# RWKV preparation with Y and Q both kept as diagonal blocks and Q's changed columns turned from Y

## The chip, the cores and the metric

The program runs on one core of a Trainium2 chip. The metric is the device time of one execution in microseconds, over several runs. The program is one launch: two layers of a trunk over 1152 tokens (1024 latent tokens and 128 context tokens), held on chip as columns, 384 tokens to a block.

## The reference, cut to what matters

Layer 1 holds a bidirectional RWKV-7 time mixing with 8 heads of 64 channels. Its scan, per head and direction, is

```python
def step(S, inp):
    r_t, w_t, k_t, v_t, kk_t, a_t = inp
    sa = jnp.einsum('bhvk,bhk->bhv', S, -kk_t)
    S = (S * w_t[:, :, None, :] + sa[..., None] * (kk_t * a_t)[:, :, None, :]
         + v_t[..., None] * k_t[:, :, None, :])
    y = jnp.einsum('bhvk,bhk->bhv', S, r_t)
    return S, y
```

The kernel computes it in chunks of 64 tokens. Inside a chunk the term `sa` makes token t depend on all earlier tokens of the chunk through a strictly triangular 64x64 matrix N (its entries are masked products of kk, a and the decay), so each chunk needs the inverse of I - N. All else in the layer around it (projections, mLSTM, norms) is matrix products and elementwise work.

## The kernel before, in words

`odd_layer_mixer` runs layer 1's two mixers. For RWKV it walks 36 steps (4 pairs of heads x 9 chunk groups). One step handles four units: two directions by two chunks of 64 tokens, with two heads on the two halves of the 128 partitions. For each step a generator `prep` (L1292) computes what does not depend on the running state, in 18 pieces divided by `yield`; `chain_block` (L1467) then carries the state. At most two `prep` generators are active, the second nine pieces behind the first. Between pieces the loop (L934 on) calls `topup`, which advances a third generator: the fills, that is the input projections of the layer, their follow-up work, and later the mLSTM. How much fill is issued between two pieces is set by a due time of 0.74 us of matmul work (`DUE`), counted by `Counted` (L53) for the fills alone; matmuls of `prep` count for nothing there. The order in which the program issues pieces is a priority and not the order of execution: the framework places each engine's instructions by readiness and its own costs when the program is closed, so a matmul of one preparation can stand among those of the other. Every matmul is recorded under L67 and every transpose under L71, so groups in the profile are told apart by their tile names.

Inside `prep` the inverse is built by doubling blocks. Y is the inverse so far (block size 1, 2, 4 ... 32), Q is its transpose. Per preparation both live in one f16 tile `YQ`, 64 columns to a unit, the heads in the two halves of the partitions. `DB[bank]` holds three f16 tiles of 128x128 diagonal blocks for the four units: N1 and N2 (the high and low parts of the triangular matrix) and QB (Q as diagonal blocks: head 0 top left, head 1 bottom right, zeros elsewhere). The pieces that concern the change:

- L1315 to L1317: Q is set to the identity. `start_inverse` (L1345): N1 is filled, and the columns that level 0 changes are copied into Q under a mask.
- L1384 to L1388: Q is copied into QB (two ACT copies, one for each half of the partitions), four matmuls with QB give Y (`i,DB` in the rows), ACT copies Y out.
- Each level l from 1 to 5, first piece: four matmuls N1 x Y (`YQ,DB`, 64 columns each), and ACT copies the product from PSUM to R (L1394).
- Each level, second piece: four matmuls QB x R (`R,DB`) give Y's new columns and eight 64x64 matmuls R x Q (`YQ,R`) give Q's. One masked copy on DVE (L1415) puts the changed half of the columns of both into YQ. Up to level 4, two ACT copies then bring Q's changed columns into QB (L1420).
- L1423 to L1431: sixteen matmuls of 64 columns form the correction I - Y + N1 Y + N2 Y; two ACT copies put it into N1 as diagonal blocks.
- L1433 to L1439: eight matmuls of 64 columns form the corrected transpose, and two ACT copies put it into PD, f32, as diagonal blocks.

Next, PD meets AT (`AT,PD`), and the results WT and EF go to the chain. A preparation has PSUM bank `sm0` or `sm1` of its own; `sm3` is shared by both, and `sm2` is the chain's.

Of the kernel before, what the change touches and what calls it, by code (L numbers as in the profile page):

```python
# [15 lines left out]
F16 = mybir.dt.float16  # L16
# [7 lines left out]
P = 128  # L24
# [61 lines left out]
def trunk_kernel(ctx: ExitStack, tc: tile.TileContext, A, outs, dbg=None, upto=99, odd="rm"):  # L86
# [7 lines left out]
    ve, sc, gp, te, sy = nc.vector, nc.scalar, nc.gpsimd, Counted(nc.tensor), nc.sync  # L94
# [13 lines left out]
    def smps(i=None):  # L108

        if i is None:  # L110
            G.turn += 1
            i = G.banks[G.turn % len(G.banks)]
        return ps_sm.tile([P, 512], F32, tag=f"sm{i}", name="sm")
# [685 lines left out]
    CH = 64  # L799
    DECAY = math.exp(-0.5)  # L800
    NCH = NT // P
    HR = [slice(0, 64), slice(64, 128)]
# [3 lines left out]
    def odd_layer_mixer(h, early):  # L806
# [19 lines left out]
        sp1 = s1.enter_context(tc.tile_pool(name="sp1", bufs=1))  # L826
        St = stage1(h, early, w_in, zm, gd, zd, zvt, zbg, zar, zbk, wend, sp1, op)
        Rw = rwkv(zd, zvt, zbg, zar, zbk, wend, y, op, fp)

        started = [0, False]  # L830
# [401 lines left out]
    def rwkv(zd, zvt, zbg, zar, zbk, wend, y, mp, fp):  # L1232
# [8 lines left out]
        i16 = mp.tile([P, CH], F16, tag="i16", name="i16")  # L1241
# [3 lines left out]
        id16 = mp.tile([P, 2, P], F16, tag="id16", name="id16")  # L1245
# [4 lines left out]
        DB = []  # L1250
        for i in range(2):
            t = mp.tile([P, 3, 4, P], F16, tag=f"DB{i}", name="DB")
            gp.memset(t, 0.0)
            DB.append(t)
        PD = mp.tile([P, 4, P], F32, tag="PD", name="PD")
        gp.memset(PD, 0.0)

        AGs = []
        for i in range(2):
            t = mp.tile([P, 4, 6, CH], F32, tag=f"AG{i}", name="AG")  # L1260
# [29 lines left out]
        def prep(n, p, i):  # L1290
            B = block_of(p, i)
            bank = n % 2  # L1292
# [9 lines left out]
            for d in range(2):  # L1302
                for hh, hr in enumerate(HR):
                    src = zvt[p][tb[d], :, hr].rearrange("(c t) v -> t c v", c=2)
# [7 lines left out]
                    gp.memset(B.XV[hr, 0::3, hh], 0.0)  # L1312


            YQ = mp.tile([P, 2, 2, 2, CH], F16, tag="YQ", name="YQ", bufs=2)  # L1315
            Y, Q = YQ[:, :, 0], YQ[:, ::-1, 1]
            sc.copy(Q, i16.unsqueeze(1).unsqueeze(1).to_broadcast([P, 2, 2, CH]))  # L1317
            yield

            GB = mp.tile([P, 4, 3, CH], F32, tag="GB", name="GB", bufs=2)  # L1320
            rights = [cols(AG, hh, PRODUCTS) for hh in range(2)]
            pgs = [smps(bank), smps(3)]
            N1, QB, N2 = (DB[bank][:, j] for j in range(3))
            lower = [GB[:, :, k] for k in ALPHA]

            def level(ap, l, first, stride, parity, dims):


                b = 1 << l
                head = [list(ap.ap[0]), [stride + (parity[1] - parity[0]) * b, 2]]  # L1330
                return bass.AP(tensor=ap.tensor, offset=ap.offset + first + parity[0] * b, ap=head + dims + [[1, b]])

            def lmask(l, hr, n):

                o = 4 * (64 - (64 >> l))
                return lm[hr, :, o : o + n * (32 >> l)].bitcast(mybir.dt.uint16)
# [8 lines left out]
            def start_inverse(hh):  # L1345
                hr = HR[hh]
                sc.copy(N1[hr, :, hr], lower[hh][hr])  # L1347
                dst = level(YQ[hr], 0, 6 * CH, -4 * CH, (1, 0), [[CH, 2], [2, 32]])[:, :, :, :, 0]
                src = level(lower[hh][hr], 0, 0, 6 * CH, (1, 0), [[3 * CH, 2], [2, 32]])[:, :, :, :, 0]
                m = lmask(0, hr, 2)[:, ::-1].rearrange("p j (c k) -> p j c k", c=2)  # L1350
                ve.copy_predicated(dst, m, src)
# [7 lines left out]
            pt = smps(3)  # L1359
            for u in range(4):  # L1360
                te.transpose(pt[:, u * P : u * P + P], BK[:, u], ident)
            for hh in (1, 0):
                start_inverse(hh)
# [4 lines left out]
                sc.copy(AG[ho, :, 5 * hh], ptv[ho, :, hr])  # L1368
            yield

            def mm2(o, lt, rt):
                for u in range(4):
                    d, c = divmod(u, 2)
                    for r_ in (slice(0, P),) if lt.shape[-1] == P else HR:
                        te.matmul(o[r_, d, c], lt[r_, u], rt[r_, d, c], start=True, stop=True)

            def halves_of(ps):
                return ps[:, : 4 * CH].rearrange("p (d c n) -> p d c n", d=2, c=2)

            def u22r(t):  # L1380
                return t.rearrange("p (d c) n -> p d c n", d=2)

            i16b = i16.unsqueeze(1).unsqueeze(1).to_broadcast([P, 2, 2, CH])
            for hr in HR:  # L1384
                sc.copy(u22r(QB)[hr, :, :, hr], Q[hr])
            py = halves_of(smps(bank))
            mm2(py, QB, i16b)
            sc.copy(Y, py)  # L1388
            yield
            for l in range(1, 6):  # L1390
                pr = halves_of(smps(bank))
                mm2(pr, N1, Y)
                R = mp.tile(U4, F16, tag="R", name="R", bufs=2)
                sc.copy(u22r(R), pr)  # L1394
                if l == 2:

                    for hh, hr in enumerate(HR):
                        gp.tensor_tensor(N2[hr, :, hr], lower[hh][hr], N1[hr, :, hr], op=OP.subtract)  # L1398
                elif l == 5:
                    pt = smps(3)  # L1400
                    for u in range(4):
                        te.transpose(pt[:, u * P : u * P + P], AG[:, u, 2:4].rearrange("p w n -> p (w n)"), ident)
                    AT = mp.tile([P, 4, P], F32, tag="AT", name="AT", bufs=1)
                    sc.copy(AT, pt.rearrange("p (u n) -> p u n", u=4))
                yield
                pyq = smps(bank)
                pyv = pyq.rearrange("p (j i c n) -> p j i c n", j=2, i=2, c=2)
                mm2(pyv[:, :, 0], QB, u22r(R))
                for u in range(4):
                    d, c = divmod(u, 2)  # L1410
                    for hr in HR:
                        te.matmul(pyv[hr, 1 - d, 1, c], R[hr, u], Q[hr, d, c], start=True, stop=True)
                dst, src = (level(t, l, 0, 4 * CH, (0, 1), [[2 << l, 4 * (32 >> l)]]) for t in (YQ, pyq))
                m = lmask(l, slice(0, P), 4).unsqueeze(3).to_broadcast([P, 2, 4 * (32 >> l), 1 << l])
                ve.copy_predicated(dst, m, src)  # L1415
                if l < 5:
                    for hr in HR:
                        nb = [2 << l, 32 >> l]
                        dst = level(QB[hr, :, hr], l, 0, 2 * P, (1, 0), [[P, 2], nb])
                        sc.copy(dst, level(YQ[hr], l, 6 * CH, -4 * CH, (1, 0), [[CH, 2], nb]))  # L1420
                yield

            pe = halves_of(smps(bank))  # L1423
            for u in range(4):
                d, c = divmod(u, 2)
                te.matmul(pe[:, d, c], id16[:, 0], i16, start=True, stop=False)
                te.matmul(pe[:, d, c], id16[:, 1], Y[:, d, c], start=False, stop=False)
                te.matmul(pe[:, d, c], N1[:, u], Y[:, d, c], start=False, stop=False)
                te.matmul(pe[:, d, c], N2[:, u], Y[:, d, c], start=False, stop=True)
            for hr in HR:  # L1430
                sc.copy(u22r(N1)[hr, :, :, hr], pe[hr])  # L1431
            yield
            pq = halves_of(smps(bank))  # L1433
            for u in range(4):
                d, c = divmod(u, 2)
                te.matmul(pq[:, d, c], id16[:, 0], Q[:, d, c], start=True, stop=False)
                te.matmul(pq[:, d, c], N1[:, u], Q[:, d, c], start=False, stop=True)
            for hr in HR:
                sc.copy(u22r(PD)[hr, :, :, hr], pq[hr])  # L1439
            yield  # L1440

            pw = smps(bank)
# [65 lines left out]
        def finish(p, i):  # L1508
# [38 lines left out]
            yield  # L1547

        R_.prep, R_.chain_block, R_.finish = prep, chain_block, finish
        return R_  # L1550

# [555 lines left out]
```

## Time and profile before

| What | us |
|---|---|
| median of 3 runs | 3409.84 |
| lowest and highest run | 3403.11, 3419.9 |
| the profiled execution | 3413.79 |
| its span, first to last instruction | 3411.7 |
| PE busy in the span | 3198.1 (94%) |
| DVE busy | 1888.0 (55%) |
| ACT busy | 1348.5 (40%) |
| POOL busy | 853.8 (25%) |

PE is the engine of the matmuls, PEld its weight loads, DVE, ACT and POOL the vector, scalar and general engines. PE's busy time is modelled and pipelined: of a run of matmuls, the distance from one start to the next is what each costs the engine, and the duration of one (about 0.19 us for 64 columns) is its latency. PEclk is the clock that was granted to PE, 1.00 being 2.4 GHz and 0.50 being 1.2 GHz. The matmuls of the preparation run from 1388 to 2460 us of the span.

### The profile page before, as it was taken

The page shows a single profiled execution, that of the slowest core. Times are in us where ns is not written, and L with a number is a line of the kernel's source. Part 1 is how long each engine was busy: PE and PEld are TensorE (multiplying, and loading weights), DVE is VectorE, ACT ScalarE, POOL GpSimd, SP SyncE. Part 2 cuts the span into 40 slices and gives each one's busy share as a digit, 9 for nine tenths or more (in the row PEclk, how much of TensorE's full clock was granted, in tenths as well). Part 3 has the DMA queues.
Part 4 walks back from the last instruction along what each step waited for, and adds up shares of the span by engine and source line. Part 5 has one row for each costly group of instructions (what it writes and reads, how often), then busy time and mean ns, then how long its engine had stood idle before and what let it go on. Part 6 is the DMA issues. An engine that isn't in the chain of part 4 may idle for free. (4 is left out here: it accounts for less than half of the span.)

```text
span 3411.7 us, 55264 instructions
## 1 busy us (share of the span) xinstructions
PE 3198.1 (94%) x21772; PEld 2939.6 (86%) x21772; DVE 1888.0 (55%) x3964; ACT 1348.5 (40%) x2864; POOL 853.8 (25%) x706
## 2 busy tenths in 40 slices
PE   7897999999999998899989899988899999999998
PEld 4775999999999997677777788877699999999998
DVE  6886655555543366567666864467856333333335
ACT  4545341112221144565665565586535111222112
POOL 2332322121111133233232431223223111111112
PEclk9998999999999999899979899999899999999999
DMA  5235412222211123444333432364251111111111
GB/s 215 91 123 174 149 48 84 92 93 87 93 50 44 44 99 112 136 108 111 102 96 105 108 95 80 107 189 137 85 188 38 44 38 44 44 44 38 44 44 75
DMA packets 255141, 315.29 MB, mean 92 GB/s; under 512 B 77138, under 2 KB 198690, under 8 KB 253346
## 3 DMA queue, kind: packets, MB, share of 16 engines
q1 hardware_dynamic: 254882, 311.77, 29.1%
q8 instruction: 171, 2.80, 0.3%
q14 instruction: 88, 0.72, 0.1%
HBM read 250.59 MB, written 61.10 MB: 91 GB/s over the span
## 5 line engine op out<-in xcount | busy, mean ns | idle before, releaser
L67 PE MATMUL mm<-h,w 128*128 128x384 f32 x8808 | 1737.8, 349 | 12.6 <-POOL w L239 4.1
L67 PEld LDWEIGHTS mm<-h,w 128*128 128x128 f32 x8808 | 1552.7, 191 | 65.1 <-issue 27.0
L67 PE MATMUL mm<-uH,w 128*128 128x384 f32 x3072 | 796.2, 338 | 0.0
L239 POOL TENSOR_TENSOR w<-w 128x1024 fp32r<-128x1024 f32 x153 | 370.6, 2422 | 1386.9 <-ACT w L238 1347.4
L238 ACT CAST w<-w 128x1024 fp32r<-128x1024 f32 x211 | 221.0, 1048 | 888.7 <-PE mm L67 843.9
L67 PEld LDWEIGHTS mm<-uH,w 128*128 128x128 f32 x3072 | 557.5, 188 | 2.5 <-issue 2.5
L376 DVE SCALAR_TENSOR_TENSOR x<-mm,mod,x 128x384 f32<-128x384 f32 (+1 forms) x576 | 282.9, 514 | 446.5 <-PE mm L67 446.0
L67 PE MATMUL mm<-uL,w 128*128 128x384 f32 x1536 | 518.0, 337 | 0.0
L396 DVE SCALAR_TENSOR_TENSOR s<-mm,r 128x384 f32<-128x384 f32 x192 | 106.8, 557 | 403.9 <-ACT r L394 403.8
L67 PEld LDWEIGHTS mm<-uL,w 128*128 128x128 f32 x1536 | 288.6, 188 | 0.0
L394 ACT ACTIVATE r<-mm 128x384 f32<-128x384 f32 x192 | 93.5, 488 | 275.2 <-PE mm L67 274.5
L239 DVE TENSOR_TENSOR uL<-s,uH 128x384 fp32r<-128x384 f32 x192 | 149.8, 781 | 87.6 <-ACT uH L238 87.2
L67 PEld LDWEIGHTS <-DB 128*128 128x128 f16 x2016 | 111.4, 101 | 77.0 <-issue 57.1
L238 ACT CAST uH<-s 128x384 fp32r<-128x384 f32 x192 | 98.5, 513 | 144.8 <-DVE s L396 144.6
L1415 DVE CAST_PREDICATED YQ<-lm,sm 128x256 f16<-128x256 uint16 x180 | 77.1, 428 | 134.8 <-PE sm L67 111.4
L196 DVE SCALAR_TENSOR_TENSOR modacc<-wmod,csl,modacc 128x512 f32<-128x512 f32 x168 | 135.3, 852 | 5.0 <-DMA wmod<-in_w_mod_dram 4.7
L1420 ACT COPY DB<-YQ 64x128 f16<-64x128 f16 x288 | 85.0, 295 | 85.0 <-DVE YQ L1415 81.1
L239 DVE TENSOR_TENSOR w<-w 128x1024 fp32r<-128x1024 f32 x58 | 82.0, 1421 | 54.9 <-ACT w L238 50.9
L67 PE MATMUL sm<-YQ,DB 128*128 128x64 f16 x1152 | 89.0, 198 | 17.6 <-DVE YQ L1415 11.7
L288 POOL TENSOR_TENSOR nacc<-nacc,nsq 128x384 f32<-128x384 f32 x56 | 66.5, 1195 | 146.8 <-ACT nsq L287 111.0
L1398 POOL TENSOR_TENSOR DB<-GB,DB 64x256 f16<-64x256 f32 x72 | 49.0, 680 | 210.4 <-ACT DB L1347 206.1
L67 PEld LDWEIGHTS sm<-XV,EF 128*128 128x128 f32 x576 | 80.0, 204 | 21.6 <-DVE EF L1456 14.9
(352 smaller groups left out, 3792.2 us busy)
## 6 DMA issues: line engine op xcount, KB each, us to landing
w<-in_mlp_w_dram SPq DMA_DIRECT2D x128, 512.0 KB
wmod<-in_w_mod_dram SPq DMA_DIRECT2D x80, 512.0 KB
w<-in_od_w_in_dram SPq DMA_DIRECT2D x31, 512.0 KB
w<-in_od_w_out_dram SPq DMA_DIRECT2D x24, 512.0 KB
BK<-zbk SPq DMA_DIRECT2D x72, 128.0 KB
AG<-zar SPq DMA_DIRECT2D x144, 64.0 KB
hbig<-zm SPq DMA_DIRECT2D x18, 512.0 KB
rb<-rowd SPq DMA_DIRECT2D x36, 256.0 KB
```

Of the source, the lines that this page charges most:

```text
L67: return self.eng.matmul(out, left, right, **kw)
L196: ve.scalar_tensor_tensor(acc[:, s], wm[:, i], c, acc[:, s], op0=OP.mult, op1=OP.add)
L238: sc.copy(Hout, src)
L239: eng.tensor_tensor(Lout, src, Hout.bitcast(F32), op=OP.subtract)
L288: (eng or (ve if tb == NTB - 1 else gp)).tensor_add(self.acc[tb], self.acc[tb], sq)
L376: ve.scalar_tensor_tensor(xs, ps[:, o], modcol(l, 2 if which == 1 else 5, m, s), xs, op0=OP.mult, op1=OP.add)
L394: sc.activation(r, ps[:, :TB], AF.Relu)
L396: ve.scalar_tensor_tensor(s, ps[:, :TB], 0.0, r, op0=OP.max, op1=OP.mult)
L1398: gp.tensor_tensor(N2[hr, :, hr], lower[hh][hr], N1[hr, :, hr], op=OP.subtract)
L1415: ve.copy_predicated(dst, m, src)
L1420: sc.copy(dst, level(YQ[hr], l, 6 * CH, -4 * CH, (1, 0), [[CH, 2], nb]))
```

## The change

Y is kept as diagonal blocks too (`YB`, 128x128 to a unit, f16), and QB is Q's only place; the tile YQ is gone. Q is set to the identity directly in QB by one 128x512 copy, and level 0's masked copy writes into QB. In each level the first piece multiplies N1 by the columns of YB that the level will change alone (again 64 columns a unit, now picked with a stride). Q's changed columns are no longer products of their own: from level 2 on, four more matmuls in the first piece (`turn`, YB as weights, columns of the identity as the moving side) transpose the columns of Y that the level before changed, into the second half of the same PSUM tile, and one ACT copy (`turned`) puts them into QB. The last level's turn stands with the correction, in bank `sm3`. The second piece keeps the four QB x R matmuls and the masked copy, of the same size as before (half of the columns of all 128 of a unit, and not half of 64 twice). The correction and the corrected transpose have 128 columns a matmul, and each is copied out by one ACT copy of 128x512 and not by two of 64x256. PD is written whole, and so the clearing of it is left out. The number of `yield`s is the same.

```diff
@@ -1253,7 +1253,6 @@
             gp.memset(t, 0.0)
             DB.append(t)
         PD = mp.tile([P, 4, P], F32, tag="PD", name="PD")
-        gp.memset(PD, 0.0)
 
         AGs = []
         for i in range(2):
@@ -1312,15 +1311,15 @@
                     gp.memset(B.XV[hr, 0::3, hh], 0.0)
 
 
-            YQ = mp.tile([P, 2, 2, 2, CH], F16, tag="YQ", name="YQ", bufs=2)
-            Y, Q = YQ[:, :, 0], YQ[:, ::-1, 1]
-            sc.copy(Q, i16.unsqueeze(1).unsqueeze(1).to_broadcast([P, 2, 2, CH]))
+
+            N1, QB, N2 = (DB[bank][:, j] for j in range(3))
+            YB = mp.tile([P, 4, P], F16, tag="YB", name="YB", bufs=2)
+            sc.copy(QB, id16[:, 0].unsqueeze(1).to_broadcast([P, 4, P]))
             yield
 
             GB = mp.tile([P, 4, 3, CH], F32, tag="GB", name="GB", bufs=2)
             rights = [cols(AG, hh, PRODUCTS) for hh in range(2)]
             pgs = [smps(bank), smps(3)]
-            N1, QB, N2 = (DB[bank][:, j] for j in range(3))
             lower = [GB[:, :, k] for k in ALPHA]
 
             def level(ap, l, first, stride, parity, dims):
@@ -1345,7 +1344,7 @@
             def start_inverse(hh):
                 hr = HR[hh]
                 sc.copy(N1[hr, :, hr], lower[hh][hr])
-                dst = level(YQ[hr], 0, 6 * CH, -4 * CH, (1, 0), [[CH, 2], [2, 32]])[:, :, :, :, 0]
+                dst = level(QB[hr, :, hr], 0, 0, 2 * P, (1, 0), [[P, 2], [2, 32]])[:, :, :, :, 0]
                 src = level(lower[hh][hr], 0, 0, 6 * CH, (1, 0), [[3 * CH, 2], [2, 32]])[:, :, :, :, 0]
                 m = lmask(0, hr, 2)[:, ::-1].rearrange("p j (c k) -> p j c k", c=2)
                 ve.copy_predicated(dst, m, src)
@@ -1368,30 +1367,44 @@
                 sc.copy(AG[ho, :, 5 * hh], ptv[ho, :, hr])
             yield
 
-            def mm2(o, lt, rt):
+            def columns(t, l, parity):
+
+                return t.rearrange("p (g k b) -> p g k b", k=2, b=1 << l)[:, :, parity]
+
+            def changed(t, l, parity):
+
+                return level(t, l, 0, 2 * P, parity, [[2 << l, 4 * (32 >> l)]])
+
+            def mm4(o, lt, rt):
                 for u in range(4):
-                    d, c = divmod(u, 2)
-                    for r_ in (slice(0, P),) if lt.shape[-1] == P else HR:
-                        te.matmul(o[r_, d, c], lt[r_, u], rt[r_, d, c], start=True, stop=True)
-
-            def halves_of(ps):
-                return ps[:, : 4 * CH].rearrange("p (d c n) -> p d c n", d=2, c=2)
-
-            def u22r(t):
-                return t.rearrange("p (d c) n -> p d c n", d=2)
-
-            i16b = i16.unsqueeze(1).unsqueeze(1).to_broadcast([P, 2, 2, CH])
-            for hr in HR:
-                sc.copy(u22r(QB)[hr, :, :, hr], Q[hr])
-            py = halves_of(smps(bank))
-            mm2(py, QB, i16b)
-            sc.copy(Y, py)
+                    r = rt(u)
+                    n = o.shape[-1] // 4
+                    te.matmul(o[:, u * n : u * n + n], lt[:, u], r, start=True, stop=True)
+
+            def by_unit(t):
+                return t.rearrange("p (u n) -> p u n", u=4)
+
+            def turn(o, l):
+
+                mm4(o, YB, lambda u: columns(id16[:, 0], l, 1 - u // 2))
+
+            def turned(o, l):
+                sc.copy(changed(QB, l, (1, 0)), o.rearrange("p (j g b) -> p j g b", j=2, b=1 << l))
+
+            H = 4 * CH
+            py = smps(bank)
+            mm4(py, QB, lambda u: id16[:, 0])
+            sc.copy(YB, by_unit(py))
             yield
             for l in range(1, 6):
-                pr = halves_of(smps(bank))
-                mm2(pr, N1, Y)
+                ps = smps(bank)
+                mm4(ps[:, :H], N1, lambda u: columns(YB[:, u], l, u // 2))
+                if l > 1:
+                    turn(ps[:, H:], l - 1)
                 R = mp.tile(U4, F16, tag="R", name="R", bufs=2)
-                sc.copy(u22r(R), pr)
+                sc.copy(R, by_unit(ps[:, :H]))
+                if l > 1:
+                    turned(ps[:, H:], l - 1)
                 if l == 2:
 
                     for hh, hr in enumerate(HR):
@@ -1403,40 +1416,29 @@
                     AT = mp.tile([P, 4, P], F32, tag="AT", name="AT", bufs=1)
                     sc.copy(AT, pt.rearrange("p (u n) -> p u n", u=4))
                 yield
-                pyq = smps(bank)
-                pyv = pyq.rearrange("p (j i c n) -> p j i c n", j=2, i=2, c=2)
-                mm2(pyv[:, :, 0], QB, u22r(R))
-                for u in range(4):
-                    d, c = divmod(u, 2)
-                    for hr in HR:
-                        te.matmul(pyv[hr, 1 - d, 1, c], R[hr, u], Q[hr, d, c], start=True, stop=True)
-                dst, src = (level(t, l, 0, 4 * CH, (0, 1), [[2 << l, 4 * (32 >> l)]]) for t in (YQ, pyq))
+                py = smps(bank)
+                mm4(py[:, :H], QB, lambda u: R[:, u])
                 m = lmask(l, slice(0, P), 4).unsqueeze(3).to_broadcast([P, 2, 4 * (32 >> l), 1 << l])
-                ve.copy_predicated(dst, m, src)
-                if l < 5:
-                    for hr in HR:
-                        nb = [2 << l, 32 >> l]
-                        dst = level(QB[hr, :, hr], l, 0, 2 * P, (1, 0), [[P, 2], nb])
-                        sc.copy(dst, level(YQ[hr], l, 6 * CH, -4 * CH, (1, 0), [[CH, 2], nb]))
+                ve.copy_predicated(changed(YB, l, (0, 1)), m, py[:, :H].rearrange("p (j g b) -> p j g b", j=2, b=1 << l))
                 yield
 
-            pe = halves_of(smps(bank))
+            pe, pt = smps(bank), smps(3)
+            turn(pt[:, :H], 5)
             for u in range(4):
-                d, c = divmod(u, 2)
-                te.matmul(pe[:, d, c], id16[:, 0], i16, start=True, stop=False)
-                te.matmul(pe[:, d, c], id16[:, 1], Y[:, d, c], start=False, stop=False)
-                te.matmul(pe[:, d, c], N1[:, u], Y[:, d, c], start=False, stop=False)
-                te.matmul(pe[:, d, c], N2[:, u], Y[:, d, c], start=False, stop=True)
-            for hr in HR:
-                sc.copy(u22r(N1)[hr, :, :, hr], pe[hr])
+                o = pe[:, u * P : u * P + P]
+                te.matmul(o, id16[:, 0], id16[:, 0], start=True, stop=False)
+                te.matmul(o, id16[:, 1], YB[:, u], start=False, stop=False)
+                te.matmul(o, N1[:, u], YB[:, u], start=False, stop=False)
+                te.matmul(o, N2[:, u], YB[:, u], start=False, stop=True)
+            turned(pt[:, :H], 5)
+            sc.copy(N1, by_unit(pe))
             yield
-            pq = halves_of(smps(bank))
+            pq = smps(bank)
             for u in range(4):
-                d, c = divmod(u, 2)
-                te.matmul(pq[:, d, c], id16[:, 0], Q[:, d, c], start=True, stop=False)
-                te.matmul(pq[:, d, c], N1[:, u], Q[:, d, c], start=False, stop=True)
-            for hr in HR:
-                sc.copy(u22r(PD)[hr, :, :, hr], pq[hr])
+                o = pq[:, u * P : u * P + P]
+                te.matmul(o, id16[:, 0], QB[:, u], start=True, stop=False)
+                te.matmul(o, N1[:, u], QB[:, u], start=False, stop=True)
+            sc.copy(PD, by_unit(pq))
             yield
 
             pw = smps(bank)
```

## Rows read from the trace of the kernel before

**Rows 1.** Three stretches: length, busy us of PE, PEld, DVE, ACT, POOL; PEclk, DMA.
```profile
0.00:1388.00 1388.00, 1303.74 (x7309) 1210.00 (x7309) 820.74 (x1317) 457.69 (x743) 347.86 (x238) 0.97 0.30 101
1388.00:2460.00 1072.00, 964.65 (x9158) 805.89 (x9158) 693.80 (x1924) 655.95 (x1732) 307.99 (x358) 0.92 0.40 111
2460.00:3411.00 951.00, 929.75 (x5306) 923.72 (x5306) 373.43 (x725) 234.91 (x390) 197.97 (x110) 0.99 0.17 59
```

**Rows 2.** PE's waits in 1388 to 2460: us in total, times, longest us.
```profile
PE sm L67 <- DVE YQ L1415: 14.0, 14, 3.9
...
PE sm L71 <- ACT AG L1368: 8.5, 10, 3.7
...
PE sm L67 <- ACT WT L1446: 5.7, 3, 4.3
PE sm L67 <- ACT R L1394: 4.9, 8, 1.2
```

**Rows 3.** PE in order of time, one level: start us, us, engine line op.
```profile
1742.18 0.29 PE L67 MATMUL sm<-YQ,DB 128*128 128x64 f16 x4
1742.31 0.78 PE L67 MATMUL mm<-h,w 128*128 128x384 f32 x3
1742.93 0.29 PE L67 MATMUL sm<-R,DB 128*128 128x64 f16 x4
1743.15 0.31 PE L67 MATMUL sm<-YQ,R 64*64 64x64 f16 x8
1743.39 0.80 PE L67 MATMUL mm<-h,w 128*128 128x384 f32 x3
```

**Rows 4.** PE in order of time, first Y (1706.67) and the sixteen of the correction (1733.33).
```profile
1706.67 0.28 PE L67 MATMUL sm<-i,DB 128*128 128x64 f16 x4
1706.78 0.60 PE L67 MATMUL mm<-h,w 128*128 128x384 f32 x2
...
1733.33 0.20 PE L67 MATMUL sm<-i,id 128*128 128x64 f16 x1
...
1733.81 0.60 PE L67 MATMUL mm<-h,w 128*128 128x384 f32 x2
```

**Rows 5.** PE in order of time, f32 matmuls of 128 columns and what follows them.
```profile
1711.66 1.16 PE L67 MATMUL sm<-AT,PD 128*128 128x128 f32 x8 [0.22 <-ACT PD L1439]
1712.65 0.28 PE L67 MATMUL sm<-R,DB 128*128 128x64 f16 x4
```

**Rows 6.** The chain that ended last, a stretch of 384-column matmuls: start us, us, what.
```profile
2477.39 73.60 PE mm L67 x408
```

**Rows 7.** Groups in 1388 to 2460: xcount | busy us, mean ns | idle before us <-releasers.
```profile
L67 PEld LDWEIGHTS <-DB 128*128 128x128 f16 x2016 | 111.4, 101 | 77.0 <-issue 57.1 <-ACT DB L1385 6.9 <-ACT DB L1420 1.2
L1420 ACT COPY DB<-YQ 64x128 f16<-64x128 f16 x288 | 85.0, 295 | 85.0 <-DVE YQ L1415 81.1 <-DVE rs_t L271 0.5
L1415 DVE CAST_PREDICATED YQ<-lm,sm 128x256 f16<-128x256 uint16 x180 | 77.1, 428 | 134.8 <-PE sm L67 111.4 <-ACT YQ L1388 7.0 <-ACT DB L1431 3.6
L1394 ACT CAST R<-sm 128x256 f16<-128x256 f32 x180 | 66.4, 369 | 59.7 <-PE sm L67 57.8
L1385 ACT COPY DB<-YQ 64x256 f16<-64x256 f16 x72 | 29.0, 403 | 11.5 <-DVE YQ L1351 10.4
L1431 ACT CAST DB<-sm 64x256 f16<-64x256 f32 x72 | 26.3, 366 | 12.8 <-PE sm L67 12.2
L1404 ACT COPY AT<-sm 128x512 f32<-128x512 f32 x36 | 20.9, 582 | 8.2 <-PE sm L71 7.8
```

**Rows 8.** ACT's copy to R and the matmuls that read it, in order of time.
```profile
1400.92 0.37 ACT L1394 CAST R<-sm 128x256 f16<-128x256 f32 x1
...
1401.34 0.28 PE L67 MATMUL sm<-R,DB 128*128 128x64 f16 x4
...
2398.94 0.36 ACT L1394 CAST R<-sm 128x256 f16<-128x256 f32 x1
...
2399.41 0.28 PE L67 MATMUL sm<-R,DB 128*128 128x64 f16 x4
```

## The prediction, made before the changed kernel was run

> **What bounds the kernel now.** I read the busy time in three stretches first. The preparations live in the middle one, 1388 to 2460 us, and nothing of the change lies outside it but one clearing of PD on POOL, so what can move is in those 1072 us. There PE is busy for 964.65 us, ACT for 655.95 and DVE for 693.80, and PE's granted clock is 0.92 of 2.4 GHz, against 0.97 and 0.99 on either side [rows 1]. So about nine tenths of the stretch are PE's own work, and matmuls of the preparation that go or grow move the end almost one to one. The rest is in PE's list of waits: those on the steps of the preparation are short and spread out, the masked copy 14.0 us, the copy of AG 8.5, of WT 5.7, of R 4.9 [rows 2]. No single wait of the inverse is worth more than that.
>
> Then I read PE in order of time, by the distance from start to start, since a single duration is latency. One level costs PE 1742.31 - 1742.18 = 0.13 us for the four N1 x Y matmuls, and 1743.39 - 1742.93 = 0.46 us for QB x R with the eight small matmuls behind it [rows 3]. Four of the 64-column kind alone cost 0.11 to 0.13, so the eight small ones with the changes of array shape around them cost 0.33 us a level. A 64-column matmul in a long run costs (1733.81 - 1733.33) / 16 = 0.030 us [rows 4].
>
> **PE's sum, for one preparation.** Before: five levels x (0.13 + 0.46) = 2.95; first Y 0.11 and correction 0.48 [rows 4]; the corrected transpose, eight of the same kind, 8 x 0.03 = 0.24. Together 3.78 us.
>
> After: level 1 is 0.13 + 0.13 = 0.26, as QB x R stands alone. Levels 2 to 5 have the four `turn` matmuls of 64 columns behind the first four: 0.13 + 4 x 0.03 + 0.13 = 0.38 each, 1.52. The last turn is 0.12. First Y, correction and corrected transpose keep their 4 + 16 + 8 = 28 matmuls but stream 128 columns and not 64. No row shows an f16 matmul of 128 columns. From below: nothing more, if each were paced by something other than its columns. From above: the f32 matmuls of 128 columns, (1712.65 - 1711.66) / 8 = 0.124 us, that is 0.094 more each [rows 5]. Between: 384 columns take 73.60 / 408 = 0.180 us [rows 6], so (0.180 - 0.030) / 320 = 0.47 ns a column, 0.030 us for 64 more, whereas 64 columns at 2.4 GHz are 0.027. I take 0.028, because it lies by the f16 row, whose 0.030 holds a whole matmul. Then 28 x 0.028 = 0.78, and the three groups cost 0.83 + 0.78 = 1.61. Sum after: 0.26 + 1.52 + 0.12 + 1.61 = 3.51.
>
> The difference is -0.27 us, times 36 preparations -10 us. With the lower end it is -1.05 a preparation (-38 us), with the upper -1.05 + 28 x 0.094 = +1.58 (+57 us).
>
> A page speaks against the middle value. The Trainium skill (TensorE: Matmul & The Clock Gate, Back-to-back issue gap) gives 81 ns a matmul for a stream of weight-load and matmul pairs at 128 columns. By that the 28 would cost 2.27 us, and the change would add 0.39 us a preparation, an estimate of +14 us. This trace has the same pairs at 64 columns 0.030 us apart [rows 4], so the weight load does not set such a pace there; no row shows 128.
>
> The moving side is now picked with a stride, in runs of 2 to 32 elements. No row shows that on PE. ACT's copies into QB and the masked copies already step that way at every level, with mean times of 295 and 428 ns and no idle of their own making [rows 7]; I add nothing. At worst the 40 strided matmuls would run at half pace, 40 x 0.03 x 36 = +43 us; a gain I exclude, since no fewer columns move.
>
> **ACT and DVE.** The masked copy has the same 256 elements a partition, 0.43 us, so DVE is unchanged. ACT before, with 0.37 us for 256 columns from PSUM, 0.40 from SBUF, 0.295 for the half-height copies of 128 columns and 0.58 for 512 from PSUM [rows 7]: Q 0.40, QB 2 x 0.40, Y 0.37, R 5 x 0.37, Q's columns 8 x 0.295, N1 and PD 4 x 0.37; 7.25 us. After: QB's identity 0.62 (0.40 plus 256 columns at (0.403 - 0.295) / 128 us), YB 0.58, R 5 x 0.37, `turned` 5 x 0.37, N1 and PD 2 x 0.58; 6.06. ACT loses 1.19 us a preparation, 43 us in all, beside PE's work: ACT is busy for 61% of the stretch. More to the point, ACT sat for 81.1 us at the head of its queue waiting for the masked copy before it could bring Q's columns into QB [rows 7]. That stall goes; the new copy waits for matmuls that stand right behind those that R waits for. What is late next is R itself, as before. Of the 8.5 + 5.7 + 4.9 = 19 us that PE waited for such ACT copies I take a fifth as won: -4 us. Zero and -19 are the ends.
>
> What stands against it: QB x R now needs R's copy and `turned` behind it. From N1 x Y to QB x R that adds the four turn matmuls, 0.12, and a copy, 0.37: 0.49 us. In 64 of 180 levels R's copy ended less than 0.65 us before its matmul started, from 1400.92 + 0.37 against 1401.34 to 2398.94 + 0.36 against 2399.41 [rows 8]; yet PE itself waited for R in 8 only. In 40 levels R's copy stood directly behind the two copies into QB (0.59 us), which leave. I book +3 us, with 0 and +42 as ends (worked out below). The start of a preparation becomes shorter (two QB copies of 0.40 leave the path, the wider YB copy adds 0.21), its end longer (0.37 + 0.58 against 2 x 0.37 before the corrected transpose); these cancel.
>
> Queues: no DMA is added or moved. The last turn takes bank `sm3` where the other preparation is in its levels and does not use it. How much fill is issued does not depend on the preparation's matmuls.
>
> Sum: -10 - 4 + 3 = -11 us against the profiled execution's 3413.79, that is 3402.8. The median of the runs is 3.95 below that execution, so I forecast 3399.
>
> **The rivals.**
> 1. *ACT's second copy decides (slower).* Of the 64 tight levels 4/5, 51, have a `turned` in front of QB x R. Each needs 0.49 us more, and the other preparation's eight small matmuls, 0.33 us of cover in between, are gone: 51 x 0.82 = +42, with PE's -10 that is +32, 3442. It turns the sign once PE waits 10 / 144 = 0.07 us more in each of the 144 levels. For it: the counts above. Against: the QB copies leave the same queue, and PE can take fill matmuls instead.
> 2. *Matmuls of 128 columns are paced by the weight load (slower).* With the 101 ns that a weight load lasts [rows 7] for each of the 28, the sum after is 1.90 + 2.83 = 4.73, +0.95 a preparation, +34 us, 3444. The page's 81 ns is the same mechanism at a lower price. Against: the 64-column pairs.
> 3. *ACT's freed queue is worth more (faster).* Half to all of the waits in [rows 2], 33 us, go as well: 3409.84 - 10 - 16 = 3383, at most 3367. For it: 81.1 us of stall at ACT's head. Against: most of PE's waits end on DVE.
> 4. *It does not save what it says.* PE's saved time comes back as waits for the masked copy, whose latency stays while the work between its ends shrinks: 3410.
>
> **How the numbers follow.** Forecast 0.44 (its own range 3389 to 3409), rival 1 0.13, rival 2 0.05, rival 3 0.24, rival 4 0.14. The range for 8 times in 10 leaves out most of rivals 1 and 2 and the far end of 3: 3374 to 3424. A measurement of this kernel tells about 0.5%, 17 us, from no change. Faster than 3393: rival 3 and the lower part of the forecast, 0.34. Slower than 3427: rivals 1 and 2, less their mild ends and with what unseen prices add, 0.17. Between: 0.49.
>
> **What would show each step.** In the profile after: the R,DB group followed at once by other work, 0.13 us; the sixteen of the correction in about 0.93 us; no ACT copy of 64x128 into DB and no wait of ACT for the masked copy ahead of it; ACT some 43 us less busy, DVE's masked copies at 428 ns; PE's waits on ACT for R and `turned` together below 10 us. PE waits of 30 us or more ahead of QB x R would prove rival 1; sixteen in 1.5 us, rival 2; a masked copy with PE waits well above 14 us, rival 4. The forecast is wrong if strided columns stream more slowly than 0.03 us a matmul, or if the new order of instructions leaves PE's clock lower than 0.92 in the stretch.

## The result, and the profile after

The changed kernel takes 3359.24 us (median of 4 runs, 3351.38 to 3369.41) against 3408.55 for the kernel before (4 runs). The ratio is 0.985, with a 95% interval of 0.982 to 0.987. The forecast was 3399 with a range from 3374 to 3424, so the sign was right and the size was not: -49 us came where -11 had been summed up. A second set of six runs of the same changed kernel, beside other runs of before, gave 3363.17 and 0.986 (0.983 to 0.989). One run of before, which took 5671 us in a slow state beside the last experiment, is left out of all that follows.

The profile page of the changed kernel, busy us, share of the span and instructions; the profiled execution took 3355.96 us:

```profile
PE 3150.0 (94%) x21052; PEld 2912.1 (87%) x21052; DVE 1888.7 (56%) x3964; ACT 1284.3 (38%) x2612; POOL 857.0 (26%) x705
```

The three stretches of the changed kernel, in the columns of [rows 1]; the preparations now end at 2403 us:

```profile
0.00:1388.00 1388.00, 1303.68 (x7309) 1211.22 (x7309) 821.09 (x1319) 459.21 (x745) 348.99 (x238) 0.97 0.30 101
1388.00:2403.00 1015.00, 918.02 (x8446) 777.88 (x8447) 697.12 (x1927) 591.23 (x1481) 306.81 (x358) 0.96 0.42 117
2403.00:3354.00 951.00, 928.26 (x5298) 923.00 (x5297) 370.52 (x720) 233.87 (x386) 201.15 (x110) 0.99 0.17 59
```

The first and last stretches are as long as before. All of the gain, 57 us of this execution, lies in the middle, 1015 us for 1072. ACT is busy 65 us less there, DVE the same within 3 us, PE 47 us less. And one column moved that the prediction had left alone: PEclk is 0.96 and was 0.92. If the clock is either 2.4 or 1.2 GHz, a mean of 0.92 is 2 x 0.08 x 1072 = 172 us at the lower level, and 0.96 is 81 us. Added up over windows of 10 us they are 167 and 78; the expectations below call this the time at half clock.

A second profile of the same changed kernel (`e8` below, an execution of 3371.05 us) tempers this:

```profile
1388.00:2416.00 1028.00, 932.60 (x8431) 790.93 (x8429) 693.95 (x1919) 589.45 (x1479) 306.05 (x355) 0.94 0.41 115
```

Its stretch lasts 1028 us at a clock of 0.94, with 120 us at half clock. PE's waits are nearly the same in both, 95 and 93 us in total, 16.3 and 16.2 of them for the masked copy. So one execution of a kernel differs from the next in clock and length while its waits stay, and a single profile says little about which edit moves the clock.

PE of the changed kernel in order of time, one level (start us, us, engine line op); it answers to [rows 3]:

```profile
1701.33 0.28 PE L67 MATMUL sm<-YB,DB 128*128 128x64 f16 x4
1701.44 0.28 PE L67 MATMUL sm<-id,YB 128*128 128x64 f16 x4
1701.56 1.29 PE L67 MATMUL mm<-h,w 128*128 128x384 f32 x6
1702.69 0.29 PE L67 MATMUL sm<-R,DB 128*128 128x64 f16 x4
1702.82 1.82 PE L67 MATMUL mm<-h,w 128*128 128x384 f32 x9
```

The first piece costs 1701.56 - 1701.33 = 0.23 us with its turn, the second 0.13: 0.36 a level, where 0.38 was booked and 0.59 was spent before. The strided moving side costs nothing that can be seen. The corrected transpose, eight f16 matmuls of 128 columns, the first, and what follows the last:

```profile
1721.42 0.22 PE L67 MATMUL sm<-DB,id 128*128 128x128 f16 x1
...
1721.87 0.28 PE L67 MATMUL sm<-YB,DB 128*128 128x64 f16 x4
```

(1721.87 - 1721.42) / 8 = 0.056 us each; booked were 0.030 for 64 columns and 0.028 for 64 more. So the open price was chosen well. The 81 ns that the Trainium skill gives (TensorE: Matmul & The Clock Gate, Back-to-back issue gap) is not seen in this trace, though every one of these matmuls has a weight load of its own.

The copies of the changed kernel in 1388 to 2403, columns as in [rows 7], and PE's waits there, as in [rows 2]:

```profile
L1422 DVE CAST_PREDICATED YB<-lm,sm 128x256 f16<-128x256 uint16 x180 | 76.7, 426 | 115.2 <-PE sm L67 113.7
L1392 ACT CAST DB<-sm 128x256 f16<-128x256 f32 x180 | 68.4, 380 | 8.6 <-PE sm L67 7.8
L1405 ACT CAST R<-sm 128x256 f16<-128x256 f32 x180 | 67.1, 373 | 111.1 <-PE sm L67 110.5
```

```profile
PE sm L67 <- DVE YB L1422: 16.3, 16, 4.1
...
PE sm L67 <- DVE DB L1350: 6.7, 8, 2.6
...
PE sm L67 <- ACT WT L1448: 5.0, 3, 3.3
PE sm L67 <- ACT DB L1392: 5.0, 8, 0.8
...
PE sm L71 <- ACT AG L1367: 1.8, 6, 0.6
```

`turned` (L1392) lasts 0.38 us, and PE waits for it 5.0 us in 8 places, as much as it waited for R before. None of the preparation's ACT copies waits for the masked copy any more. But ACT's stall has mostly moved and not gone: the copy to R now stands 110.5 us waiting for PE, where it stood 57.8 [rows 7]. Before, these two copies waited 81.1 + 57.8 = 139 us; now R and `turned` wait 110.5 + 7.8 = 118. Of the 19 us that PE waited for AG, WT and R, 1.8 + 5.0 + 5.0 = 12 are left.

### The profile page after: what moved, and what is told of

Same layout as the page of the kernel before. It is cut to its first block, busy times and chain, and to the rows that moved or that the text cites. A ratio compares the mean times of both kernels' runs of the same rounds, so it can differ in the third digit from the quotient of the medians.

```text
span 3354.2 us, 53476 instructions
## 1 busy us (share of the span) xinstructions
PE 3150.0 (94%) x21052; PEld 2912.1 (87%) x21052; DVE 1888.7 (56%) x3964; ACT 1284.3 (38%) x2612; POOL 857.0 (26%) x705
## 4 chain that ended last, share of the span: by engine, by line
PE 70%; DVE 15%; ACT 5%; issue 3%; POOL 2%; DMA 1%; SPq 0%; DVEq 0%; POOLq 0%; ACTq 0%
PE mm L67 59%; PE sm L67 8%; PE ex L67 2%; DVE GB L1341 1%; DVE AG L1342 1%; PE sm L71 1%; DVE xc L1200 1%; DMA AG<-zar 1%; DVE DB L1350 1%; DVE YB L1422 1%; ACT h L363 1%; DVE xc L605 1%; DVE nt L360 0%; DVE rs_t L271 0%; POOL ii L636 0%
## 5 line engine op out<-in xcount | busy, mean ns | idle before, releaser
L67 PE MATMUL mm<-h,w 128*128 128x384 f32 x8808 | 1715.8, 347 | 10.6 <-POOL w L239 3.7
L67 PEld LDWEIGHTS <-DB 128*128 128x128 f16 x2016 | 121.7, 101 | 76.9 <-issue 46.2
L1422 DVE CAST_PREDICATED YB<-lm,sm 128x256 f16<-128x256 uint16 x180 | 76.7, 426 | 115.2 <-PE sm L67 113.7
L1405 ACT CAST R<-sm 128x256 f16<-128x256 f32 x180 | 67.1, 373 | 111.1 <-PE sm L67 110.5
L67 PE MATMUL sm<-YB,DB 128*128 128x64 f16 (+1 forms) x1008 | 91.2, 205 | 13.5 <-DVE YB L1422 12.0
L67 PE MATMUL sm<-XV,EF 128*128 128x64 f32 x576 | 83.2, 284 | 15.7 <-DVE EF L1458 13.3
```

The lines of the kernel that those rows point to most:

```text
L67: return self.eng.matmul(out, left, right, **kw)
L1405: sc.copy(R, by_unit(ps[:, :H]))
L1422: ve.copy_predicated(changed(YB, l, (0, 1)), m, py[:, :H].rearrange("p (j g b) -> p j g b", j=2, b=1 << l))
```

## The experiments

Two theories of the missing 38 us stood first. *Small matmuls*: the eight 64x64 matmuls of each level had held PE's clock down. *ACT queue*: the stall and the copies that left ACT had made PE wait, and those waits had let the clock fall. Four kernels were to tell them apart. The edits are cut to the lines that matter.

**Before without the small matmuls** (`e1`).

```diff
-mm2(pyv[:, :, 0], QB, u22r(R))
-    te.matmul(pyv[hr, 1 - d, 1, c], R[hr, u], Q[hr, d, c], ...)
+    te.matmul(pyv[:, d, :, c], QB[:, u], R[:, u].unsqueeze(1).to_broadcast([P, 2, CH]), ...)
```

> The kernel before, with the eight 64x64 matmuls of each level left out; the four QB x R matmuls write 128 columns instead (each product twice), so Q gets Y's values and the output is not the reference's. ACT's two copies into QB stay. PE's sum: 0.33 us less and 4 x 0.028 more a level, -0.22 x 180 = -40 us. Theory 'small matmuls' (they held PE's granted clock down): the time at half clock in the stretch of the preparations falls from 166 us to about 80 as in the changed kernel, another -40: about 3330. Theory 'ACT queue' (the stall and the copies on ACT made PE wait, and the waits made the clock fall): only the sum, about 3370, half-clock time still about 166 us.

3367.59 us (4 runs), 0.988 (0.984 to 0.991) of before: -45 us, between the two expectations and near the bare sum of -40. The granted clock of a whole run rose from 0.9637 to 0.9682 (means over runs).

**Before with Q's copies on DVE** (`e2`).

```diff
-sc.copy(dst, level(YQ[hr], l, 6 * CH, -4 * CH, (1, 0), [[CH, 2], nb]))
+ve.tensor_copy(dst, level(YQ[hr], l, 6 * CH, -4 * CH, (1, 0), [[CH, 2], nb]))
```

> The kernel before, with the two copies of Q's changed columns into QB on DVE, right behind the masked copy, and not on ACT; same output. Theory 'ACT queue': ACT's stall of 81 us and 85 us of its work are gone, so most of the gain beyond PE's own sum appears: 3365 to 3375, half-clock time well under 166 us. Theory 'small matmuls': PE's work is unchanged, 3400 to 3412, half-clock time about 166 us.

3418.29 us (10 runs), 1.002 (1.000 to 1.004). To take work and stall off ACT gains nothing here, where DVE takes on 81 us of copies in turn. That speaks against the ACT theory in its plain form.

**Changed kernel with ACT's copies and stall put back** (`e3`).

```diff
 ve.copy_predicated(changed(YB, l, (0, 1)), m, ...)
+if l < 5:
+    for hr in HR:
+        sc.copy(SCR[hr].rearrange("p (j n) -> p j n", j=2), YB[hr, 0::2, hr])
```

> The changed kernel, with two ACT copies of 64x128 behind the masked copy of levels 1 to 4, from YB into a tile that nothing reads: ACT's stall and its work of before come back, all else stays; same output. Theory 'ACT queue': 35 to 45 us of the gain are lost, 3395 to 3405. Theory 'small matmuls': 3357 to 3368.

3374.51 us (4 runs), 0.989 (0.986 to 0.993): 11 us above the six runs of the changed kernel. The stall is back in its list of ACT's waits, yet it costs about a quarter of what the theory wanted:

```profile
ACT SCR L1423 <- DVE YB L1420: 65.8, 59, 6.0
```

**Changed kernel with the small matmuls put back** (`e4`).

```diff
 mm4(py[:, :H], QB, lambda u: R[:, u])
+for u in range(4):
+    for hr in HR:
+        te.matmul(py[hr, H + u * CH : H + u * CH + CH], R[hr, u], QB[hr, u, hr], ...)
```

> The changed kernel, with the eight 64x64 matmuls R x Q of each level put back behind QB x R, into the free half of the bank, which nothing reads; same output. PE's sum: +0.33 x 180 = +59 us. Theory 'small matmuls': the half-clock time goes from 78 back to about 166 us as well, +40 more, about 3455. Theory 'ACT queue': the sum alone, 3410 to 3420, half-clock time about 80 us.

3422.19 us (10 runs), 1.003 (1.000 to 1.005): +59 us over the changed kernel's six runs by the medians, as summed up. The clock fell only from 0.971 to 0.968, so *small matmuls* falls as the main account of the clock.

The removal seemed priced well, and the added columns had been measured at their price in the trace. So I looked at the runs themselves. Within one and the same kernel the time follows the granted clock: of 62 runs of before, the fastest is 3391.94 us at 0.970 and the slowest 3427.02 at 0.956. Over 154 runs in 14 sets of one kernel each, every run against the mean of its set, the slope is -25.6 us for 0.01 of clock, and taking it out shrinks the scatter from 6.5 to 2.3 us. So each kernel can be read twice, as it ran and at the clock of before. That a slope found within kernels also holds between them is assumed. For it speak the two profiles of the changed kernel, which differ in clock and length while PE's waits hardly do. The chip matters little: the four groups of runs of before, one to a chip, have means from 3408 to 3415 us as they ran and from 3411 to 3413 at equal clock. The last three columns come from the one profiled execution of each set: the stretch from 1388 us to the end of the preparations, PE's idle time in it (its length less PE's busy time) and the time at half clock.

| Kernel | runs | median us | mean clock | mean us at 0.9637 | stretch us | PE idle us | half clock us |
|---|---|---|---|---|---|---|---|
| before | 62 | 3411.2 | 0.9637 | 3411.2 | 1072 | 107 | 167 |
| changed, first set | 4 | 3359.2 | 0.9720 | 3381.1 | 1015 | 97 | 78 |
| changed, second set | 6 | 3363.2 | 0.9710 | 3381.6 | 1028 | 95 | 120 |
| e1 before, no small matmuls | 4 | 3367.6 | 0.9682 | 3379.2 | 1021 | 111 | 113 |
| e2 before, Q's copies on DVE | 10 | 3418.3 | 0.9650 | 3422.3 | 1082 | 109 | 160 |
| e3 changed, ACT copies back | 4 | 3374.5 | 0.9707 | 3392.6 | 1034 | 106 | 102 |
| e4 changed, small matmuls back | 10 | 3422.2 | 0.9684 | 3433.4 | 1082 | 90 | 129 |
| e5 changed, more columns | 12 | 3399.9 | 0.9720 | 3421.5 | 1060 | 102 | 107 |
| e6 before, more columns | 12 | 3419.8 | 0.9704 | 3437.4 | 1077 | 99 | 107 |
| e7 changed, old start | 6 | 3373.9 | 0.9710 | 3393.8 | 1031 | 106 | 96 |
| e9 before, twice the columns | 6 | 3437.8 | 0.9738 | 3464.3 | 1097 | 99 | 88 |
| e10 changed, old ACT parts | 7 | 3389.2 | 0.9677 | 3401.0 | 1045 | 109 | 116 |
| e11 before, new start | 6 | 3386.6 | 0.9690 | 3399.4 | 1032 | 94 | 87 |
| e12 changed, more on POOL | 5 | 3363.3 | 0.9740 | 3390.5 | 1022 | 101 | 85 |

Read at equal clock, e4 stands 52 us above the changed kernel and not 59: some 7 of its 59 us are clock. The time at half clock, by which the expectations would tell the theories apart, tells little from one profile: it is 78 us in one profile of the changed kernel and 120 in the other, and e3 to e7 lie between these two or within 9 us of them.

A new theory came of it: full-array columns, which the change adds, lift the clock and so pay for part of themselves; and the start of a preparation, booked at nothing, was worth something. The next four kernels ran on one chip; the first is the second set named above.

> The changed kernel unaltered, so that the others of this call have it on their chip: about 3359.

**More columns in the changed kernel** (`e5`).

```diff
 mm4(py[:, :H], QB, lambda u: R[:, u])
+for u in range(4):
+    te.matmul(py[:, H + u % 2 * P : H + u % 2 * P + P], QB[:, u], id16[:, 0], ...)
```

> The changed kernel, with four more full-array f16 matmuls of 128 columns behind QB x R in each level, into the free half of the bank, which nothing reads; same output. 20 x 0.056 us x 36 = +40 us at full clock. Theory 'columns cost what they last': +36 to +44 over the changed kernel, and the sum of the prediction failed elsewhere. Theory 'full-array columns come cheap' (they partly stand in waits, and PE's clock falls less often with them): +10 to +28, with the time at half clock below that of the changed kernel (78 us).

3399.92 us (12 runs): +37 us over the changed kernel on the same chip. Here columns cost about what they last, 40 us at equal clock; the theory fails for this kernel.

**More columns in the kernel before** (`e6`).

```diff
 mm2(pr, N1, Y)
+for u in range(4):
+    te.matmul(pr_[:, (2 + u % 2) * P : (3 + u % 2) * P], N1[:, u], id16[:, 0], ...)
```

> The kernel before, with four more full-array f16 matmuls of 128 columns behind N1 x Y in each level, into the free half of the bank, which nothing reads; same output. Theory 'columns cost what they last': +36 to +44, about 3450. Theory 'full-array columns come cheap': 3420 to 3438, with the time at half clock well below 166 us.

3419.82 us (12 runs), 1.003 (1.001 to 1.005): 40 us of matmuls cost 9. The stretch of the preparations in this kernel, columns as in [rows 1]:

```profile
1388.00:2465.00 1077.00, 978.42 (x9877) 820.96 (x9877) 691.53 (x1920) 655.71 (x1730) 306.53 (x357) 0.95 0.40 110
```

PE has 14 us more busy time than before, five more of the stretch, and a clock of 0.95 where it was 0.92. At equal clock the columns cost 26 us, and the clock gave 17 back. They stand behind N1 x Y here and behind QB x R in e5, so what differs between the two is the place as well as the kernel.

**The old start in the changed kernel** (`e7`).

```diff
-sc.copy(QB, id16[:, 0].unsqueeze(1).to_broadcast([P, 4, P]))
+Q0 = YB[:, :, :CH]
+sc.copy(Q0, i16.unsqueeze(1).to_broadcast([P, 4, CH]))
...
+for hr in HR:
+    sc.copy(QB[hr, :, hr], Q0[hr])
 mm4(py, QB, lambda u: id16[:, 0])
```

> The changed kernel, with the start of before: Q's identity and level 0 in a tile of 64 columns (the part of YB that is free until then), and two ACT copies of it into QB ahead of the first Y; same output. It puts 0.8 us of ACT copies back into each preparation's path. If the start is what the prediction missed, +15 to +25 us over the changed kernel; as the prediction booked it, 0 to +6.

3373.93 us (6 runs): +11 us, and +12 at equal clock. More than was booked, less than the whole miss. PE is idle for 106 us of the stretch, against 95 in e8.

**Twice the columns in the kernel before** (`e9`): `range(8)` for `range(4)` in e6.

> The kernel before, with eight (not four) more full-array f16 matmuls of 128 columns behind N1 x Y in each level, which nothing reads; same output. Four of them cost +9 us and raised the mean granted clock from 0.963 to 0.971. Theory 'the lift of the clock is used up': the next four cost what they last or nearly, +30 to +40 over the run with four, about 3455, clock 0.970 to 0.974. Theory 'every column lifts it': +5 to +15 over the run with four, about 3430, clock 0.977 or more.

3437.83 us (6 runs), 1.009 (1.007 to 1.012): 23 us over e6 by the ratios. At equal clock each four cost the same, 26 and 27 us; the clock rose by 0.007 with the first and by 0.003 with the second. The lift fades. The clock of 0.974 is what the first theory expected, the time lies between the two.

**Both ACT parts of before in the changed kernel** (`e10`): e3 and e7 together, but with Q's identity written by two ACT copies of 64 rows where e7 has one of 128.

> The changed kernel with both of the parts of before that were put back singly: the two ACT copies behind the masked copy (into a tile that nothing reads) and the old start. Same output. If they are two effects: +11 + 11 = +22 over the changed kernel, about 3385. If both are one (ACT's queue is full either way): +11 to +16, about 3376.

3389.19 us (7 runs), 0.995 (0.993 to 0.997): +26 us by the medians, +19 at equal clock. That is nearer to two effects (+22) than to one (+11 to +16), though at equal clock it is less than e3's 11 and e7's 12 together.

**The new start in the kernel before** (`e11`).

```diff
 sc.copy(Q, i16.unsqueeze(1).unsqueeze(1).to_broadcast([P, 2, 2, CH]))
+sc.copy(DB[bank][:, 1], id16[:, 0].unsqueeze(1).to_broadcast([P, 4, P]))
...
+ve.copy_predicated(dst2, m, src)
 ve.copy_predicated(dst, m, src)
...
-for hr in HR:
-    sc.copy(u22r(QB)[hr, :, :, hr], Q[hr])
```

> The kernel before, with the start of the changed one: the identity goes straight into QB, level 0's masked copy writes QB as well (a second masked copy on DVE, 0.38 us for each head), and the two ACT copies of 0.40 us ahead of the first Y are gone. Same output. If the shorter start is worth what it was worth in the changed kernel: -6 to -12, 3399 to 3405, with the granted clock unchanged at 0.963. If it is worth nothing here: 3408 to 3416.

3386.58 us (6 runs), 0.994 (0.992 to 0.996). That is -20 us, and the expectation was -6 to -12 with the clock unchanged: -12 at equal clock, the price that e7 gave from the other side, and the rest with a clock that rose to 0.969. The gain comes although ACT still writes the old identity too and DVE makes 72 more masked copies. The stretch in this kernel:

```profile
1388.00:2420.00 1032.00, 938.00 (x9147) 782.27 (x9147) 703.68 (x1987) 642.70 (x1691) 305.85 (x355) 0.96 0.41 115
```

**More off ACT's queue** (`e12`), an attempt to beat both kernels.

```diff
-sc.copy(QB, id16[:, 0].unsqueeze(1).to_broadcast([P, 4, P]))
+gp.tensor_copy(QB, id16[:, 0].unsqueeze(1).to_broadcast([P, 4, P]))
-sc.copy(N1[hr, :, hr], lower[hh][hr])
+gp.tensor_copy(N1[hr, :, hr], lower[hh][hr])
```

> The changed kernel, with two more things taken off ACT's queue: POOL writes the identity into QB (0.62 us a preparation) and casts the triangular matrix into N1 (2 x 0.40 us, ahead of which ACT stood for 50 us waiting for DVE's masks). Same output. Theory 'a stall at ACT's head is worth its share' (the stall behind the masked copy, put back, cost 11 us): -5 to -14 against the changed kernel, about 3351. Against it: POOL's queue has weight splits of 2.4 us, and N1 and the level-0 columns behind them may come late, 0 to +15 us.

3363.33 us (5 runs), 0.985 (0.983 to 0.988), the same as the changed kernel. It ran at a higher clock, and at equal clock it is 9 us worse. So POOL's copies, 0.68 and 2 x 0.41 us, gain nothing in place of ACT's. No version here beats the changed one.

## Why the prediction was wrong

**PE's sum, -10 us: borne out at equal clock.** e10 is the changed kernel without its two gains on ACT; at the clock of before it stands at 3401.0 against 3411.2, that is -10, though `turned` and the longer end of a preparation are in this too, and by the medians as they ran it is -22. The parts hold roughly: 59 us were booked for the small matmuls, which cost 59 as they ran and 52 at equal clock (e4), and 40 for four columns' matmuls a level, which cost 37 and 40 in the changed kernel (e5). In the kernel before, e6 got the same columns for 9 and 26, which the sum has no term for.

**"These cancel", the start and the end of a preparation: wrong.** The start was worth 11 to 12 us, shown from both sides by e7 and e11; the longer copies at the end were not tried by themselves. I had set the durations of copies against each other, which says nothing of what PE loses by them. The loss shows as PE's idle time: 106 us with the old start in the changed kernel against 97 and 95 without, 94 with the new start in the kernel before against 107. ACT's load is not the measure, since e3 gives ACT 85 us more busy time than e8 and e7 only 21, and both lose 11 us. How the shorter start saves it stays open. Two copies into QB no longer stand between DVE's level-0 copy and the first Y, with 10.4 us of ACT's idle time put down to that copy [rows 7]; but PE's own wait just ahead of the first Y is not shorter, 6.7 us for DVE's copy (L1350, above) where it was 3.4 for ACT's:

```profile
PE sm L67 <- ACT DB L1385: 3.4, 3, 2.0
```

**ACT's stall, -4 us: too small.** e3 gives 11 us, inside the ends that were named. That it was not a matter of ACT's load alone, e2 and e12 suggest: less work for ACT, given to DVE or POOL, gained nothing. And "that stall goes" was only partly so: 118 of the 139 us in which those copies waited are still there.

**The +3 us for `turned`, and rival 1: did not come.** PE's wait ahead of QB x R stayed at 5.0 us, in 8 of 180 levels. So a copy that ends shortly before its matmul does not mean that PE stands idle for it. Rival 2 fell with the 0.056 us, rival 4 with the gain that came. Rival 3 came nearest, but for a part of its reason only, and even its far end, 3367, was passed.

**The clock: the term that the sum lacked.** I carried 0.92 over as a constant and named only its fall as a danger. From before to the changed kernel the whole run went from 0.9637 to 0.971, and by the slope of the runs that is 0.0073 x 2560 = 19 us. So the 48 us between the medians 3411.2 and 3363.2 part into about 10 for PE's sum, 19 for the two ACT parts and 19 for the clock. They add up because they are steps down one table (before, e10, changed, each at equal clock, then the clock), so the closing of this sum proves nothing; the shares rest on the slope, which is 26.7 us for 0.01 from before's runs alone and 23.6 from all the others. What raises the clock is shown in part: the added columns alone do in the kernel before (e6), the new start alone does (e11), and putting both ACT parts back takes about 0.003 away (e10), whereas put back singly (e3, e7) they take nothing that can be told. Those shares don't add up to one account, so which edit lifted it in the changed kernel stays open; whether e1's rise came from the small matmuls that left or from the columns that stood in for them was not tried either.

## What to carry to other kernels

Where a stretch runs at a mean granted clock well below 1, book the clock as a term of its own: look at the runs of one kernel for the slope of time against clock, and ask of each edit whether it fills PE's waits or makes them. What a copy costs is not read from its engine's load: here two copies of 0.40 us at the start were worth 11 us, as much as eight of 0.295 us behind the masked copies, and 1.4 us a preparation given from ACT to POOL nothing. And compare kernels at equal clock too before deciding what an edit's own work costs, and profile a kernel twice before trusting the clock of one stretch.

## What the runs showed of the hardware

The spread of this kernel's runs, about 1% from end to end, goes almost wholly with the granted clock: 25.6 us for 0.01, with 2.3 us of scatter left. In the changed kernel PE waited for the masked copy just before one such fall; PE in order of time, and the busy time of the stretches about it:

```profile
1712.17 0.22 PE L67 MATMUL sm<-id 128*128 128x128 f16 x1 [2.19 <-DVE YB L1422]
...
1715.44 1.31 PE L67 MATMUL mm<-h,w 128*128 128x384 f32 x3
1716.55 0.65 PE L67 MATMUL sm<-id,DB 128*128 128x128 f16 x4
```

```profile
1700.00:1712.00 12.00, 9.52 (x79) 7.61 (x80) 9.37 (x12) 6.60 (x17) 6.90 (x7) 1.00 0.49 138
1712.00:1719.00 7.00, 6.10 (x33) 5.49 (x33) 6.11 (x14) 4.73 (x11) 2.86 (x5) 0.52 0.48 117
1719.00:1728.00 9.00, 9.00 (x96) 7.69 (x94) 5.95 (x9) 6.77 (x16) 5.27 (x5) 0.99 0.28 66
```

After 2.19 us of waiting the clock averages 0.52 over the next 7 us, which is the 1.2 GHz level for nearly all of them, and three fill matmuls of 384 columns take 1716.55 - 1715.44 = 1.11 us there, 0.37 each, against 0.18 at full clock [rows 6]: there the work behind a wait pays for it again. It need not. In the same execution PE then stands still for a longer time, busy for 0.40 of 3 us, and the clock stays at 1.00 through the 7 us behind:

```profile
1728.00:1731.00 3.00, 0.40 (x4) 0.28 (x3) 2.78 (x8) 0.07 (x1) 1.00 (x4) 1.00 0.83 198
1731.00:1738.00 7.00, 7.00 (x56) 6.12 (x57) 3.90 (x9) 2.82 (x8) 1.38 (x2) 1.00 0.35 101
```

The other surprise was how much 40 us of matmuls that nobody reads may cost: 9 us in a kernel whose PE is idle for 107 us of the stretch and runs at 0.92, 37 in one where it is idle for 97 us and runs at 0.96. Whether the kernel or the place of the matmuls in a level makes this difference was not tried.
